# The last two of 22 inner column tiles of a feed-forward block, computed by rows and turned by transposing transfers

## The chip, the cores and the metric

One core of one Trainium2 chip runs the whole program in one launch. The metric is the device time of one execution in microseconds; the kernel before has a median of 1212.53 us over three runs (1212.32 to 1212.62). The engines named below are TensorE (PE, with its weight loads as PEld), VectorE (DVE), ScalarE (ACT), GpSimd (POOL) and SyncE (SP), which issues most transfers from memory.

## The reference, cut to what matters

The trunk has two layers of three sub-blocks each, on 256 tokens of width 1024, all in float32. Two sub-blocks of each layer are feed-forward blocks (FFNs), four in all:

```python
def _swiglu(x, w1, w3, w2):
    return (jax.nn.silu(x @ w1) * (x @ w3)) @ w2

for l in range(DEPTH):
    h = _swiglu(x, ffn_w1[l, 0], ffn_w3[l, 0], ffn_w2[l, 0])
    x = _layernorm(ALPHA * x + 0.5 * h, ln_g[l, 0], ln_b[l, 0])
    ...
```

`w1` and `w3` are 1024 x 2816 and `w2` is 2816 x 1024. The inner width of 2816 is 22 tiles of 128 columns. The mixer between the two FFNs isn't touched by the change.

## The kernel before, in words

Every float32 product is made of three products in a reduced 32-bit format (fp32r): each operand is cut into a high part (a copy on ScalarE) and a low part (operand minus high part, on VectorE), and high x high, high x low and low x high are summed in a bank of PSUM. Weights come from memory in loads of 1 MB (128 partitions x 2048 numbers) on SP's queue, into a ring of four buffers named `raw`. `stream` (L155) issues one such load, and cuts it in two pieces of 1024 columns into a ring of eight high (`whi`) and eight low (`wlo`) buffers. `step` numbers the loads; the number is the priority by which a planner puts the instructions of all engines but TensorE in order, and `behind(ins)` lets an instruction stand only after `ins` on its engine. TensorE runs in the order written. All engines take their instructions in the planned order.

A first matrix is computed in one of two ways:

- By rows (`gemm_rows`, L406): 128 tokens of x are the stationary operand and 512 columns of weights stream past, so tokens lie on partitions. Five blocks of four tiles each (20 of the 22 tiles) go this way. A block has 96 matmuls of 512. Its result h = silu(x w1) * (x w3) has to be turned, because the second matrix needs the inner dimension on partitions: `front` (L695) makes Silu on ScalarE and the product on VectorE, ScalarE splits the 32-bit words in two planes of 16 bits (`planes`, L702), SP issues a transposing transfer (L704) into `turned`, and `columns` (L681) later joins the planes on ScalarE (L688) and cuts the result into high and low parts (`keep`, L673).
- By columns (`gemm_a2`, L273): 128 columns of weights are the stationary operand and x streams past, the high and low part side by side in 512 columns; so the result lies turned already. High weights take 512 columns (x high and x low, L283), low weights 256 (x high, L290). ScalarE copies one half of each bank out (L291), VectorE adds it to the other (L293); then come Silu (L721) and the product (L722). The last two tiles (20 and 21) go this way in the loop at L717, with all four `side` banks, and their `keep` follows at once.

The second matrix (L740 on) sums over the 22 tiles of h in pairs. Five pairs (tiles 4 to 13) go through a seven-product scheme with combined weights (`stream_s`, L340: S0 to S4 in this text, seven products of three matmuls on seven banks); VectorE and ScalarE make the combinations and their high (`shi`) and low (`slo`) parts. The pairs (0,1) and (2,3) are plain loads (`plain_pair`, L732: P0 and P1), computed behind S0 and S1. The last four pairs, tiles 14 to 21, are held until the end, when the banks of the output are finished one by one: 24 matmuls of 512 for each. TensorE's order is S0, P0, S1, P1, S2, S3, S4, held. The layer norm (`Norm`) follows; two row vectors of it are fetched once one element of the last h tile is written (L505).

Of the kernel before, what the change touches and what calls it, by code (L numbers as in the profile page):

```python
# [11 lines left out]
F32 = mybir.dt.float32  # L12
# [28 lines left out]
EPS = 1e-5  # L41
# [17 lines left out]
def trunk(ctx, tc, x, xT, w13a, w13b, w2s, w2p, wb, wqk, wa, wbr, wo, gateb, sgug, sgub, sguwT, sgubias, lam, diffg,  # L59
# [18 lines left out]
    def name(s):  # L78
        serial[0] += 1
        return f"{s}_{serial[0]}"  # L80
# [21 lines left out]
    def t512(s, n=2):  # L102
        return tmp.tile([P, 512], F32, tag="main", name=name(s), bufs=n)

    def s512(s, n=4):
        return tmp.tile([P, 512], F32, tag="side", name=name(s), bufs=n)
# [39 lines left out]
            for task in list(tasks):  # L146
                turn(task)

    latest, added, emptied, silu, turned_by, early = [None, None], [None], [None], [None], [None], [None]

    def behind(ins):

# [2 lines left out]
    def stream(src, width=CH, sub=HC, lent=(), after=(None, None)):  # L155

        step()
        raw = raw_pool.tile([P, CH], F32, tag="raw", name=name("raw"))  # L160
        nc.sync.dma_start(raw[:, :width], src)
        out = []
        for o in range(0, width, HC):
            if o // HC in lent:
                hi, lo = ([act.tile([P, 512], F32R, tag="slot", name=name(n)) for _ in range(2)] for n in ("lhi", "llo"))
                at = [(hi[j], lo[j]) for j in range(2)]
            else:
                hi = hi_pool.tile([P, HC], F32R, tag="hi", name=name("whi"))
                lo = lo_pool.tile([P, HC], F32R, tag="lo", name=name("wlo"))
                at = [(hi[:, p : p + sub], lo[:, p : p + sub]) for p in range(0, HC, sub)]  # L170
            for p, (h, w) in zip(range(0, HC, sub), at):
                r = raw[:, o + p : o + p + sub]
                with behind(latest[0] if o // HC in lent else early[0] or latest[0]):
                    copied = A.activation(h, r, AF.Copy)  # L174
                if o // HC in lent:
                    early[0] = copied.ins
                with behind(after[o // HC] or latest[1]):
                    V.tensor_tensor(out=w, in0=r, in1=h.bitcast(F32), op=ALU.subtract)  # L178
            out.append((hi, lo))
        return out  # L180
# [470 lines left out]
    def ffn(l, f, i, norm, following=None):  # L651
# [21 lines left out]
        def keep(q, qa):  # L673
            if q in SQ:
                mixed(q, qa)
            else:
                split(p_hi[q], p_lo[q], qa)
# [3 lines left out]
        def columns(ins):  # L681
            while waiting:
                k0, tt = waiting.pop(0)
                h = tmp.tile([P, 2, 512], F32, tag="columns", name=name("columns"), bufs=1)
                to = h.bitcast(U16).rearrange("p q (k u t w) -> p (q k) u t w", k=2, u=2, w=2)
                for t in range(NT):
                    with behind(ins):
                        A.activation(to[:, :, t], tt[:, t].bitcast(U16).rearrange("p (w c t) -> p c t w", w=2, c=FB),  # L688
                                     AF.Copy)
                for j in range(2):  # L690
                    keep((k0 + 2 * j, k0 + 2 * j + 1), h[:, j])
                if norm is None and k0 == 0:
                    beside(setup(h[:, 0, :1]), 0)

        def front(k0):  # L695
# [12 lines left out]

            return rows

        if norm is None:
            gemm_first([w13b[l, f, 0, 0], w13b[l, f, 1, 0]], front(0))
        else:
            gemm_b2([w13b[l, f, 0, 0], w13b[l, f, 1, 0]], xh, xl, front(0), norm=norm)
        for n in range(1, NB):
            gemm_rows([w13b[l, f, m, n] for m in range(2)], xh, xl, front(n * FB), (bank, side_bank)[n % 2])
        for j in range(FR, FT, 2):  # L717
            qa = s512("qa")
            for m, z in gemm_a2([w13a[l, f, j - FR + m] for m in range(2)], both, lambda m: t512("silu"), bank=side_bank):
                s = z[:, :T]  # L720
                silu[0] = A.activation(s, s, AF.Silu).ins  # L721
                V.tensor_tensor(out=qa[:, m * T : (m + 1) * T], in0=s, in1=z[:, T:], op=ALU.mult)  # L722
                columns(silu[0])
            keep((j, j + 1), qa)
        ln = Norm(l, i, 2.0 * ALPHA, 4.0 * EPS, qa[:, :1], last)
        S = {n: side_bank() for n in (3, 7, 4)}
        S.update({n: bank() for n in (1, 2, 5, 6)})
        ends = {(0, 0): [(S[2], 0, 512)], (0, 1): [(S[3], 0, 512)], (1, 0): [(S[4], 0, 512)],
# [11 lines left out]
        for n, q in enumerate(SQ):  # L740
            pair, w = stream_s(w2s[l, f, n], pair)
            for b in (1, 2, 5, 6, 3, 7, 4):
                three(S[b], *s_op[q][b], *w[b], n == 0, n == NS - 1 and b in (1, 5, 6, 7))
            beat(1.75)
            if n < len(PQ) - HELD:
                plain_pair(n)
        u, v = s512("u"), s512("v")
        A.activation(u, S[6], AF.Copy)
        for m in range(HELD // 2):
# [265 lines left out]
def _layout(i):  # L1015
    c = np.ascontiguousarray
    L = DEPTH
    f = {k: np.asarray(v) for k, v in i.items()}
    x = f["x"].reshape(T, D)
    o = {"x": x, "xT": c(x.reshape(T, KT, P).transpose(2, 1, 0)).reshape(P, KT * T)}  # L1020

    def cols(w):

        k, n = w.shape[-2:]
        w = w.reshape(*w.shape[:-2], k // P, P, n // P, P)
        a = w.ndim
        return w.transpose(*range(a - 4), a - 2, a - 3, a - 4, a - 1)

    def pairs(w):

        w = cols(w)
        lead = w.shape[:-4]
        n = w.shape[-4]
        w = w.reshape(*lead, n // 2, 2, P, KT, P)
        a = w.ndim
        return c(w.transpose(*range(a - 4), a - 3, a - 4, a - 2, a - 1)).reshape(*lead, n // 2, P, CH)

    def halves(w):

        k, n = w.shape[-2:]  # L1040
        w = w.reshape(*w.shape[:-2], k // P, P, n // 512, 512)
        a = w.ndim
        w = c(w.transpose(*range(a - 4), a - 2, a - 3, a - 4, a - 1))
        return w.reshape(*w.shape[:-2], (k // P) * 512)

    nb = FR * P
    w1, w3 = f["ffn_w1"], f["ffn_w3"]
    o["w13a"] = c(np.stack([cols(w1[..., nb:]), cols(w3[..., nb:])], axis=4)).reshape(L, 2, FT - FR, P, CH)
    o["w13b"] = c(np.stack([halves(w1[..., :nb]), halves(w3[..., :nb])], axis=2))
    w2 = f["ffn_w2"].reshape(L, 2, FT, P, 2, 512)  # L1050

    def blocks(at):

        return c(np.stack([w2[:, :, k, :, h] for k, h in at], axis=3)).reshape(L, 2, P, CH)

    o["w2s"] = c(np.stack([blocks(((a, 0), (a, 1), (b, 1), (b, 0))) for a, b in SQ], axis=2))
    now, late = PQ[: len(PQ) - HELD], PQ[len(PQ) - HELD :]
    o["w2p"] = c(np.stack([blocks(((a, 0), (b, 0), (a, 1), (b, 1))) for a, b in now]
                          + [blocks([(k, h) for q in late[2 * m : 2 * m + 2] for k in q])
                             for h in range(2) for m in range(HELD // 2)], axis=2))  # L1060
    u, v, q, k, val, ga, gb = (f["w_in"][:, :, s * D : (s + 1) * D] for s in range(7))
    o["wb"] = np.stack([halves(w) for w in (v, val)], axis=1)
    o["wqk"] = np.stack([pairs(w) for w in (q, k)], axis=2)
    o["wa"] = np.stack([pairs(w) for w in (u, ga, gb)], axis=1)
    o["wbr"] = pairs(f["w_branch"])
    o["wo"] = halves(f["w_out"])
    o["gateb"] = c(f["gate_b"].reshape(L, 2, KT, P).transpose(3, 0, 1, 2))
    o["sgug"], o["sgub"] = f["sgu_ln_g"], f["sgu_ln_b"]
    o["sguwT"] = c(f["sgu_w"].transpose(0, 3, 1, 2)).reshape(L, P, GROUPS * P)
    o["sgubias"] = f["sgu_b"].reshape(L, GROUPS * P)  # L1070
    o["lam"] = f["lam"]
    o["diffg"] = c(f["diff_ln_g"].T)
    o["lng"], o["lnb"] = f["ln_g"], f["ln_b"]
    for k in ("lng", "lnb"):
# [26 lines left out]
```

## Time and profile before

| what | value |
|---|---|
| median of three runs | 1212.53 us |
| the profiled execution | 1213.05 us |
| its span in the trace | 1211.3 us |
| TensorE busy | 1203.7 us (99%), 5961 matmuls |
| VectorE busy | 942.9 us (78%) |
| ScalarE busy | 857.4 us (71%) |
| DMA engines, main queue | 59.9% of 16 engines |

A row of a group of instructions reads: line, engine, operation, output <- inputs, shape, count | busy time in all, mean ns of one | idle time of the engine just before, and what ended it. In a timeline, the first two numbers are start and length in us, and a bracket tells idle time before it and what ended it. A matmul's recorded length is from its issue to its end; since matmuls overlap, what one costs is the distance of starts.

### The profile page before, as it was taken

The numbers are of one execution on the slowest core, as the hardware profiler recorded it, in microseconds if no ns is written. First come the engines' busy times: TensorE is split into PE (matmuls) and PEld (weight loads), VectorE is DVE, ScalarE is ACT, GpSimd is POOL, SyncE is SP. The second block draws the span as 40 slices with busy tenths as digits, with TensorE's granted clock in tenths as the row PEclk, the third lists the DMA queues.
The fourth block names the chain that finished last, engine by engine and source line by source line (L and its number), as shares of the span: only waits on it lengthen the run. The fifth ranks groups of instructions, "written<-read, shape, count | busy, mean of one in ns | idle before, by whom it ended". The sixth has DMA issues, their size and how long they took to land.

```text
span 1211.3 us, 16542 instructions
## 1 busy us (share of the span) xinstructions
PE 1203.7 (99%) x5961; PEld 1011.3 (83%) x5961; DVE 942.9 (78%) x1540; ACT 857.4 (71%) x1384; POOL 91.1 (8%) x184
## 2 busy tenths in 40 slices
PE   9999999999999999999999999999999999999998
PEld 8888888888888878888888888888888888888886
DVE  6658998885696876579985679989766877757797
ACT  7677677679865595776776776776898556867761
POOL 0100000233300000000000000003331000000000
PEclk9999999999999999999999999999999999999999
DMA  8985665655764658665668665766648456677551
GB/s 321 323 261 174 211 249 208 227 177 166 232 227 164 217 178 282 191 192 218 229 216 270 195 176 207 254 223 199 213 139 273 176 174 217 201 259 210 184 202 47
DMA packets 101346, 257.00 MB, mean 212 GB/s; under 512 B 66528, under 2 KB 67600, under 8 KB 74640
## 3 DMA queue, kind: packets, MB, share of 16 engines
q1 hardware_dynamic: 97296, 243.03, 59.9%
q0 software_dynamic: 3536, 12.13, 3.2%
q8 instruction: 46, 0.75, 0.3%
q10 hardware_dynamic: 432, 0.79, 0.2%
q14 instruction: 36, 0.29, 0.1%
HBM read 235.47 MB, written 1.05 MB: 195 GB/s over the span
## 4 chain that ended last, share of the span: by engine, by line
PE 91%; DVE 4%; ACT 3%; issue 1%; DMA 0%; SPq 0%; POOL 0%; DVEq 0%; ACTq 0%; POOLq 0%
PE bank L271 35%; PE sbank L271 24%; PE bank L283 16%; PE bank L290 8%; PE sbank L283 2%; PE bank L446 2%; PE sbank L290 1%; PE sbank L829 1%; DVE wlo L178 1%; PE sbank L961 1%; ACT pp L839 0%; DVE nwa L248 0%; ACT xf L638 0%; ACT whi L174 0%; PE sbank L878 0%
## 5 line engine op out<-in xcount | busy, mean ns | idle before, releaser
L178 DVE TENSOR_TENSOR wlo<-raw,whi 128x1024 fp32r<-128x1024 f32 (+1 forms) x396 | 436.6, 1125 | 144.5 <-ACT whi L174 113.9
L174 ACT ACTIVATE whi<-raw 128x1024 fp32r<-128x1024 f32 (+1 forms) x396 | 372.9, 971 | 124.4 <-PE bank L283 43.2
L271 PE MATMUL bank<-whi,x 128*128 128x512 f32 x840 | 263.3, 390 | 0.0
L271 PEld LDWEIGHTS bank<-whi,x 128*128 128x128 f32 x840 | 157.7, 188 | 32.9 <-DVE gz L293 0.2
L271 PE MATMUL bank<-wlo,x 128*128 128x512 f32 x420 | 163.5, 389 | 0.0
L271 PE MATMUL sbank<-whi,x 128*128 128x512 f32 x512 | 158.9, 389 | 0.0
L283 PE MATMUL bank<-x,whi 128*128 128x512 f32 x640 | 156.0, 394 | 0.0
L283 PEld LDWEIGHTS bank<-x,whi 128*128 128x128 f32 x640 | 117.1, 188 | 26.3 <-issue 2.3
L271 PEld LDWEIGHTS sbank<-whi,x 128*128 128x128 f32 x512 | 96.1, 188 | 20.0
L353 ACT ACTIVATE shi<-raw 128x1024 fp32r<-128x1024 f32 (+1 forms) x80 | 73.4, 946 | 51.7 <-DVE raw L368 26.4
L271 PE MATMUL sbank<-wlo,x 128*128 128x512 f32 x256 | 99.6, 389 | 0.0
L355 DVE TENSOR_TENSOR slo<-raw,shi 128x1024 fp32r<-128x1024 f32 (+1 forms) x80 | 85.4, 1088 | 14.1 <-ACT shi L353 13.3
L271 PEld LDWEIGHTS bank<-wlo,x 128*128 128x128 f32 x420 | 78.9, 188 | 16.0
L290 PE MATMUL bank<-x,wlo 128*128 128x256 f32 x640 | 85.9, 285 | 0.0
L290 PEld LDWEIGHTS bank<-x,wlo 128*128 128x128 f32 x640 | 81.6, 191 | 2.2
L291 ACT ACTIVATE r<-bank 128x256 f32<-128x256 f32 x112 | 41.6, 377 | 24.0 <-PE bank L290 24.0
L271 PEld LDWEIGHTS sbank<-wlo,x 128*128 128x128 f32 x256 | 48.1, 188 | 9.9
L271 PE MATMUL sbank<-whi,hhi 128*128 128x512 f32 x144 | 56.3, 391 | 0.0
L271 PE MATMUL sbank<-whi,hlo 128*128 128x512 f32 x144 | 56.1, 390 | 0.0
L271 PE MATMUL sbank<-wlo,hhi 128*128 128x512 f32 x144 | 56.0, 389 | 0.0
L506 POOL DMA_DIRECT2D bc<-in_lng x6 | 3.2, 530 | 696.2 <-DVE bc L505 696.2
L702 ACT ACTIVATE planes<-silu 128x1024 uint16<-128x1024 uint16 x40 | 42.0, 1053 | 7.3 <-DVE silu L701 6.2
(247 smaller groups left out, 1999.1 us busy)
## 6 DMA issues: line engine op xcount, KB each, us to landing
raw<-in_w13b SPq DMA_DIRECT2D x76, 1024.0 KB, 5.4
raw<-in_w2p SPq DMA_DIRECT2D x24, 1024.0 KB, 4.9
raw<-in_wa SPq DMA_DIRECT2D x24, 1024.0 KB, 5.4
raw<-in_w2s SPq DMA_DIRECT2D x20, 1024.0 KB, 4.9
raw<-in_wb SPq DMA_DIRECT2D x16, 1024.0 KB, 5.3
raw<-in_wqk SPq DMA_DIRECT2D x16, 1024.0 KB, 4.8
raw<-in_wbr SPq DMA_DIRECT2D x16, 1024.0 KB, 4.9
raw<-in_w13a SPq DMA_DIRECT2D x8, 1024.0 KB, 4.8
```

The costliest lines, as they stand in the source:

```text
L174: copied = A.activation(h, r, AF.Copy)
L178: V.tensor_tensor(out=w, in0=r, in1=h.bitcast(F32), op=ALU.subtract)
L271: PE.matmul(ps, xx, w, start=start and n == 0, stop=stop and n == 2)
L283: PE.matmul(b[-1], hi[:, k * P : (k + 1) * P], xc(k), start=k == 0, stop=False)
L290: PE.matmul(b[n][:, :T], lo[:, k * P : (k + 1) * P], xc(k)[:, :T], start=False, stop=k == KT - 1)
L291: emptied[0] = A.activation(r[:, s], b[n][:, T:], AF.Copy, scale=scale).ins
L353: A.activation(h, r, AF.Copy)
L355: V.tensor_tensor(out=w, in0=r, in1=h.bitcast(F32), op=ALU.subtract)
L446: PE.matmul(ps[t][m], x[:, j, o + t * P : o + (t + 1) * P], y, start=k0 + j == 0 and o == 0 and y is hi, stop=k0 + j == KT - 1 and y is lo)
L702: A.activation(pk.rearrange("p (w k) -> p w k", w=2), s.bitcast(U16).rearrange("p (k w) -> p w k", w=2), AF.Copy)
L829: PE.matmul(banks[m][:, j * nk : (j + 1) * nk], rows(qT, m, j, t * P, P), rows(kT, m, j, 0, nk), start=True, stop=True)
L961: PE.matmul(b[:, j * T + t * P : j * T + (t + 1) * P], vg[t][:, g // 4, s], wsT[g // 4][:, s], start=True, stop=True)
```

## The change

Tiles 20 and 21 are computed by rows too. Their weights are laid out anew: 256 columns of w1 and 256 of w3 side by side, so that one bank of 512 holds both for 128 tokens. A function `narrow` takes the place of the loop: two loads of 1 MB as before, 48 matmuls of 512 on two side banks, then for each half of the tokens a Silu of 256 columns, a product, a plane split and a transposing transfer of half the size of a row block's. `columns` learns to take a turned tile of one pair, and the step for the last pair is called within the second matrix after P1, behind the last copy of P1 on ScalarE (`copied`). The joins of tiles 16 to 19 come behind the Silu of the second half of the tokens, where they came behind the Silu of tile 20. The norm's row vectors hang on the new `s`.

```diff
@@ stream @@
                 with behind(latest[0] if o // HC in lent else early[0] or latest[0]):
-                    copied = A.activation(h, r, AF.Copy)
+                    done = A.activation(h, r, AF.Copy)
+                copied[0] = done.ins
@@ columns @@
                 k0, tt = waiting.pop(0)
+                nq = 2 if k0 < FR else 1
                 h = tmp.tile([P, 2, 512], F32, tag="columns", name=name("columns"), bufs=1)
-                to = h.bitcast(U16).rearrange("p q (k u t w) -> p (q k) u t w", k=2, u=2, w=2)
+                to = h[:, :nq].bitcast(U16).rearrange("p q (k u t w) -> p (q k) u t w", k=2, u=2, w=2)
                 for t in range(NT):
                     with behind(ins):
-                        A.activation(to[:, :, t], tt[:, t].bitcast(U16).rearrange("p (w c t) -> p c t w", w=2, c=FB),
-                                     AF.Copy)
-                for j in range(2):
+                        A.activation(to[:, :, t], tt[:, t, : nq * T].bitcast(U16).rearrange("p (w c t) -> p c t w",
+                                                                                             w=2, c=2 * nq), AF.Copy)
+                for j in range(nq):
                     keep((k0 + 2 * j, k0 + 2 * j + 1), h[:, j])
@@ ffn @@
+        def narrow():
+
+            tt = act.tile([P, 2, 512], F32, tag="val", name=name("turned"), bufs=2)
+            ps = [side_bank() for _ in range(NT)]
+            for c in range(2):
+                for n, piece in enumerate(stream(w13a[l, f, :, c * CH : (c + 1) * CH])):
+                    for t in range(NT):
+                        rows_b(ps[t], t, 4 * c + 2 * n, piece, xh, xl, KT)
+            for t in range(NT):
+                s, pk = t512("silu"), s512("planes")[:, :T].bitcast(U16)
+                silu[0] = A.activation(s[:, :T], ps[t][:, :T], AF.Silu).ins
+                V.tensor_tensor(out=s[:, :T], in0=s[:, :T], in1=ps[t][:, T:], op=ALU.mult)
+                planes(pk, s[:, :T])
+                nc.sync.dma_start_transpose(out=tt[:, t, :T].bitcast(U16).rearrange("p (c t) -> p c t", c=4), in_=pk)
+            columns(silu[0])
+            waiting.append((FR, tt))
+            return s
...
-        for j in range(FR, FT, 2):
-            qa = s512("qa")
-            for m, z in gemm_a2([w13a[l, f, j - FR + m] for m in range(2)], both, lambda m: t512("silu"), bank=side_bank):
-                s = z[:, :T]
-                silu[0] = A.activation(s, s, AF.Silu).ins
-                V.tensor_tensor(out=qa[:, m * T : (m + 1) * T], in0=s, in1=z[:, T:], op=ALU.mult)
-                columns(silu[0])
-            keep((j, j + 1), qa)
-        ln = Norm(l, i, 2.0 * ALPHA, 4.0 * EPS, qa[:, :1], last)
+        s = narrow()
+        ln = Norm(l, i, 2.0 * ALPHA, 4.0 * EPS, s[:, :1], last)
...
             if n < len(PQ) - HELD:
                 plain_pair(n)
+            if n == len(PQ) - HELD - 1:
+                columns(copied[0])
@@ _layout @@
-    o["w13a"] = c(np.stack([cols(w1[..., nb:]), cols(w3[..., nb:])], axis=4)).reshape(L, 2, FT - FR, P, CH)
+    o["w13a"] = halves(np.concatenate([w1[..., nb:], w3[..., nb:]], axis=-1))[:, :, 0]
```

More of the change, by code (lines that the diff above doesn't have):

```diff
@@ L147, in finish_tasks @@
                 turn(task)
-    latest, added, emptied, silu, turned_by, early = [None, None], [None], [None], [None], [None], [None]
+    latest, added, emptied, silu, turned_by, early, copied = [None, None], [None], [None], [None], [None], [None], [None]
     def behind(ins):
@@ L173, in stream @@
                 with behind(latest[0] if o // HC in lent else early[0] or latest[0]):
-                    copied = A.activation(h, r, AF.Copy)
+                    done = A.activation(h, r, AF.Copy)
+                copied[0] = done.ins
                 if o // HC in lent:
-                    early[0] = copied.ins
+                    early[0] = done.ins
                 with behind(after[o // HC] or latest[1]):
```

## The prediction

> **What bounds the kernel now.** I read the page's busy times first, then TensorE's list of waits, then the chain that ended last around the edited stage, then busy time by window.
>
> ```profile
> span 1211.3 us, 16542 instructions
> PE 1203.7 (99%) x5961; PEld 1011.3 (83%) x5961; DVE 942.9 (78%) x1540; ACT 857.4 (71%) x1384; POOL 91.1 (8%) x184
> ```
>
> ```profile
> PE sbank L458 <- DVE warm L454: 1.0, 1, 1.0
> PE sbank L588 <- DVE xtok L574: 1.0, 1, 1.0
> PE sbank L633 <- DVE xtok L556: 0.8, 2, 0.4
> PE bank L271 <- DVE x L234: 0.5, 3, 0.2
> PE sbank L592 <- ACT minus L590: 0.2, 1, 0.2
> ```
>
> TensorE is busy 1203.7 of 1211.3 us, and all its recorded waits are 3.5 us: 1.0 at the warm-up, 1.2 in the last norm, and 0.8 + 0.5 = 1.3 us in the middle, all at norms. No wait belongs to the edited stage. So the time is the number of columns that TensorE streams, plus a fixed part for each matmul.
>
> The chain through the second of the four feed-forward blocks (FFN 2) shows the stage. Columns are start, length, what:
>
> ```profile
> 493.04 21.76 PE sbank L271 x96
> 514.80 21.76 PE bank L271 x96
> 536.56 7.25 PE sbank L283 x32
> 543.82 3.83 PE sbank L290 x32
> 547.65 0.47 PE bank L271 x2
> ```
>
> The first two rows are row blocks of four tiles (96 matmuls of 512), on either set of banks. The next two are the column stage that the change replaces: 32 matmuls of 512 with the high weights and 32 of 256 with the low ones. The last row is the start of the second matrix. By window, all four stages look alike, three of them shown (PE, PEld, DVE, ACT, POOL busy, clock, DMA share, GB/s); the last two rows are the stages after it, in FFN 2:
>
> ```profile
> 114.74:125.82 11.08, 11.08 (x65) 9.83 (x65) 9.82 (x16) 9.91 (x13) 0.00 (x0) 1.00 0.50 143
> 536.56:547.65 11.09, 11.09 (x66) 9.84 (x65) 9.83 (x16) 9.91 (x13) 0.00 (x0) 1.00 0.47 143
> ...
> 1135.53:1146.62 11.09, 11.09 (x65) 9.84 (x65) 9.83 (x16) 9.91 (x13) 0.00 (x0) 1.00 0.51 144
> 547.65:582.36 34.71, 34.71 (x154) 28.73 (x154) 34.17 (x42) 22.61 (x29) 1.05 (x2) 1.00 0.57 206
> 553.73:578.70 24.97, 24.97 (x112) 20.69 (x111) 24.56 (x27) 15.10 (x17) 0.00 (x0) 1.00 0.57 206
> ```
>
> TensorE is full in all of them, at clock 1.00. But from 553.73 to 578.70 VectorE is nearly full too (24.56 of 24.97 us): this is the one place near the edit where another engine could take over. ScalarE has 9.9 us to spare there, the DMA engines 43%.
>
> **TensorE, part by part.** Removed: 4 x 11.09 (once 11.08) = 44.35 us. Added per block: two loads x two halves x two token halves x two k x three products = 48 matmuls of 512, in the same order and form as a row block, so 48 x 21.76/96 = 48 x 0.2267 = 10.88 us; four times, 43.52. The streamed columns are equal (32 x 512 + 32 x 256 = 48 x 512 = 24,576). What goes is the fixed part of 16 matmuls. From the two column rows, 7.25/32 = 226.6 ns for 512 and 3.83/32 = 119.7 ns for 256 give 0.4176 ns a column and 12.8 ns fixed; 16 x 12.8 = 0.205 us a block, which agrees with 11.09 - 10.88 = 0.21. **Term: -0.83 us.** The price is bounded closely, since both sets of banks ran row blocks in 21.76.
>
> The Trainium skill, "TensorE: Matmul & The Clock Gate", section "Wait — 56ns, not 53.3ns?", gives a warm matmul N columns at 2.4 GHz plus about 2.5 ns; by that the 16 matmuls would be worth 0.04 us a block and the sum -0.16. The rows above disagree (226.6 ns, where it has 215.7), and I go by the rows.
>
> **The read-outs.** Durations by form, over the whole kernel:
>
> ```profile
> L688 ACT ACTIVATE columns<-turned 128x1024 uint16<-128x1024 uint16 x40 | 44.9, 1171 | 0.0
> L702 ACT ACTIVATE planes<-silu 128x1024 uint16<-128x1024 uint16 x40 | 42.0, 1053 | 7.3 <-DVE silu L701 6.2
> ...
> L233 ACT ACTIVATE hhi<-columns 128x512 fp32r<-128x512 f32 x20 | 12.5, 623 | 0.0
> ...
> L291 ACT ACTIVATE r<-sbank 128x256 f32<-128x256 f32 x16 | 6.0, 375 | 0.0
> ...
> L721 ACT ACTIVATE silu<-silu 128x256 f32<-128x256 f32 x8 | 3.4, 419 | 1.0 <-DVE silu L293 1.0
> ```
>
> ```profile
> L293 DVE TENSOR_TENSOR silu<-sbank,r 128x256 f32<-128x256 f32 x16 | 6.4, 420 | 0.0
> ...
> L722 DVE TENSOR_TENSOR qa<-silu 128x256 f32<-128x256 f32 x8 | 3.4, 420 | 0.0
> L234 DVE TENSOR_TENSOR hlo<-qa,hhi 128x512 fp32r<-128x512 f32 x4 | 2.8, 691 | 0.1
> ```
>
> VectorE per block: four additions and two multiplications go (6 x 0.42 = 2.52), two multiplications come (0.84): **-1.68 us**, and the 0.69 of the low half of h moves to a later place. ScalarE: four copies and two Silu go (1.50 + 0.84 = 2.34); two Silu (0.84), two plane splits and two joins of 128x512 in 16 bits come. No row has a 16-bit copy of 512; it lies between half of the 1024 rows (0.53 and 0.59) and all of them (1.05 and 1.17); I take 0.62, by the copy of equal element count. So 0.84 + 4 x 0.62 = 3.3, **+1.0 us** (ends +0.7 and +2.9). Neither is on the path, because TensorE waits for neither now; the cover is tested below.
>
> Banks: the column stage fills all four side banks and the second matrix asks for them back; the row stage fills two, read out by the same time. Weight buffers: a column load's low halves are used only from 543.82 on, so their buffers come free last; by rows a pair is freed every 2.72 us. The last high half stays 10.88 - 7.25 = 3.6 us longer; the first low half goes 7.25 + 3.83/4 - 2.72 = 5.5 us sooner. VectorE's 0.5 us wait for such a low buffer (below) should shrink. Loads: the two weight loads now have a row stride, as the row blocks' have (5.4 us to land, where this one has 4.8); both were issued within 4.94 us of 501.69, and TensorE first used them at 536.56, so 0.6 us is hidden.
>
> ```profile
> 501.69 4.94 SPq L161 DMA_DIRECT2D raw<-in_w13a  x2
> ```
>
> ```profile
> raw<-in_w13b SPq DMA_DIRECT2D x76, 1024.0 KB, 5.4
> ...
> raw<-in_w13a SPq DMA_DIRECT2D x8, 1024.0 KB, 4.8
> ...
> turned<-planes SPq DMA_TRANSPOSE x40, 3.9
> ```
>
> **The moved step.** The last pair's columns now go Silu, product, planes, two transposing transfers on SP's queue, two joins on ScalarE, high copy, low difference; the last four wait until P1 has been copied (the second matrix's loads come in the order S0, P0, S1, P1, S2, S3, S4; S is a combined load, P a plain one). TensorE's last row matmul would end near 547.4; with 0.3 for the release, Silu, product and planes (0.42 + 0.42 + 0.62) the second transfer is ready near 549.3, or near 553 if the previous block's joins (2 x 1.17 and two high copies, 1.25) go first. On SP's queue the next loads of the second matrix stood at 547.91 and 556.20:
>
> ```profile
> 547.91 0.33 SPq L344 DMA_DIRECT2D raw<-in_w2s  x1
> ...
> 556.20 0.33 SPq L344 DMA_DIRECT2D raw<-in_w2s  x1
> ```
>
> Ahead of the first, the transfers would delay it by about 2 us; that load was not copied before 556.7, so it has that time. Landing took 3.9 us in the median, so the joins can run from 553.2 or, at the late end, from 556.9; the copies of P1 ended at 556.8 (554.82 + 1.99). The pair itself is needed at the earliest late in the 24 held matmuls after 582.36, some 25 us on. What matters is what stands behind the joins on ScalarE: copies for S2, then S3 and S4, and with them VectorE's chain.
>
> ```profile
> 554.82 1.99 ACT L174 ACTIVATE whi<-raw 128x1024 fp32r<-128x1024 f32 x2
> 556.71 2.27 ACT L353 ACTIVATE shi<-raw 128x512 fp32r<-128x512 f32 x3
> ```
>
> ```profile
> 544.81 1.23 DVE L178 TENSOR_TENSOR wlo<-raw,whi 128x1024 fp32r<-128x1024 f32 x1 [0.49 <-PE sbank L290]
> ...
> 558.36 2.42 DVE L355 TENSOR_TENSOR slo<-raw,shi 128x512 fp32r<-128x512 f32 x3
> ...
> 576.20 2.52 DVE L355 TENSOR_TENSOR slo<-raw,shi 128x1024 fp32r<-128x1024 f32 x2
> ```
>
> ```profile
> 579.70 0.39 PE L271 MATMUL bank<-slo,shh 128*128 128x512 f32 x1
> ```
>
> The tightest point is S4's last low half: ready at 576.20 + 2.52 = 578.72, used at 579.70, **0.98 us of slack**. The joins put 2 x 0.62 + 0.62 = 1.86 us on ScalarE ahead of S2. If all of it came through, TensorE would wait 1.86 - 0.98 = 0.88 us a block, 3.5 in all; with joins at the long end (1.17 each) 2.96 - 0.98 = 2.0 a block, 7.9 in all. Against it stand VectorE's 1.68 us less work ahead and ScalarE's 9.9 us of idle time. At the other end, a gain, the earlier VectorE could remove the 1.3 us of waits at norms. I take 0, since the relief is about as large as the delay and the slack comes on top.
>
> **Sum.** -0.83 us. The profiled execution took 1213.05 us (span 1211.3 and 1.75 around it), so 1212.22; it ran 0.52 above the median 1212.53, so beside that **1211.7 us**, 0.07% less. What a measurement of this kernel can tell from no change is about 0.2%, or 2.4 us.
>
> **Rivals.**
>
> *The chain of low halves slips a little.* The 3.5 us above without relief: 1212.53 - 0.83 + 3.5 = 1215.2. For it: VectorE 98% busy from 553.73. Against it: the 1.68 us.
>
> *ScalarE is held by the transfer: slower.* In the view of the norm's turned tile, ScalarE did stand still for such a landing, 1.0 us each of five times:
>
> ```profile
> L628 ACT ACTIVATE xf<-sent x10: 1180/1186/1190, 180.8 to 1038.3; 128x1024 uint16<-128x1024 uint16 x10
> its engine sat idle before it (us, times) until:
>   DMA sent<-planes: 5.0, 5
> ```
>
> If the transfers are queued behind the load at 556.20, they land 0.33 + 3.9 later, at 560.4; the joins and high copy end at 562.3, S2's first copy (half a load, 0.6) at 562.9, where VectorE began at 558.36: 4.5 late, less 0.98, 3.5 us of TensorE waiting a block, 14.2 in all: **1225.9**. It decides once the delay passes 0.98 us, and counts as slower (over 0.2%) from (2.4 + 0.83)/4 = 0.8 more. Against it: the planes are ready 3 to 7 us before that load goes out, so a planner has no cause to put them behind it. The Trainium skill speaks against the change here: the same page, section "Architectural detail: the array is 16× 32×32, not 1× 128×128", has ScalarE take its instructions strictly in order. The five waits agree with that.
>
> *The norms' waits go too:* -0.83 - 1.3 = -2.1, **1210.4**. For it: less VectorE work before them. Against it: those waits hang on the norm's own steps, 45 us later.
>
> *The fixed part isn't saved:* the 12.8 ns is worked out from two forms, and might be the price of the 256 form alone; then 1212.5. Against it: both row blocks ran their 96, each with its own load, in 21.76.
>
> **Chances.** Forecast 0.68; fixed part not saved 0.06; norms too 0.06; small slip 0.09, half of it over 0.2%; held ScalarE 0.05; not foreseen 0.06, of which 0.04 faster. Faster by over 0.2%: 0.04; slower: 0.045 + 0.05 + 0.02, taken as 0.12; within: 0.84. The likeliest's own range is 1211.3 to 1212.2; the one asked for reaches from the norms' case to the small slip, 1210.4 to 1215.2.
>
> **What would show it.** Right: the four stages last 10.88 us with 48 matmuls of 512; TensorE's waits stay near 3.5 us with none on low halves of S2 to S4; the first matmul of the second matrix comes 0.21 us sooner in each block; the low halves of P0 come before 544.8. Wrong: a wait of TensorE on VectorE or ScalarE after the stage, ScalarE idle for the turned tile, S4's low half later than 0.98 us before its use, or a row stage of other than 10.88 us. A change over 2.4 us either way contradicts the sum.

## The result, and the profile after

The changed kernel takes 1216.56 us in the median of 7 runs (1215.46 to 1219.69). The kernel before took 1212.78 us in the median of 7 runs on the same chip (1212.32 to 1213.84). The ratio is 1.0032, with a 95% interval of 1.0022 to 1.0041: slower by 3.8 us, where 0.8 us less was forecast. The profiled execution took 1215.97 us, for a span of 1214.2.

The first lines of the page after, then TensorE's waits (engine, line, what it waited for: us in total, times, longest):

```profile
span 1214.2 us, 16393 instructions
PE 1204.3 (99%) x5897; PEld 1007.7 (83%) x5897; DVE 935.8 (77%) x1524; ACT 861.4 (71%) x1384; POOL 90.7 (7%) x184
```

```profile
PE bank L272 <- DVE slo L356: 1.7, 2, 0.9
...
PE sbank L589 <- DVE xtok L575: 1.0, 1, 1.0
PE sbank L634 <- DVE xtok L557: 0.8, 2, 0.4
PE sbank L844 <- ACT sbank L901: 0.7, 1, 0.7
```

TensorE has 64 matmuls fewer, VectorE 7 us less to do and ScalarE 4 us more, as forecast. Two waits are new: 1.7 us for low halves of the second matrix (slo), and 0.7 us for a bank in a mixer, far from the edit.

The chain through FFN 2 (start, length, what), and the windows of the four stages by rows (length; PE, PEld, DVE, ACT, POOL busy; clock; DMA share; GB/s):

```profile
537.10 10.88 PE sbank L272 x48
547.98 2.72 PE bank L272 x12
```

```profile
114.85:125.73 10.88, 10.88 (x49) 9.01 (x49) 10.75 (x17) 7.57 (x9) 0.00 (x0) 1.00 0.56 157
537.10:547.98 10.88, 10.88 (x50) 9.01 (x49) 10.75 (x17) 7.57 (x9) 0.00 (x0) 1.00 0.56 156
...
1135.62:1146.50 10.88, 10.88 (x50) 9.01 (x49) 10.75 (x17) 7.57 (x9) 0.00 (x0) 1.00 0.61 157
```

The stage does what it was to do: 10.88 us each time, with TensorE full. So the loss is elsewhere. Each part of the program starts with the same matmul in every kernel, so the starts in two traces can be subtracted part by part. The table is worked out in this way. It gives the length of each part in the profiled execution of before (the last part ends with TensorE's last matmul), and the difference of each other kernel to it; the experiments' names are explained below (e3, e6, e7 and e8, which aren't in the table, are told in the text).

| part, by before's time (us) | before | after | e1 | e2 | e4 | e5 | e9 | e10 | e11 |
|---|---|---|---|---|---|---|---|---|---|
| start, to 27.5 | 27.54 | +.11 | -.02 | -.32 | -.24 | -.33 | -.34 | +.43 | -.35 |
| FFN 1, to 178.4 | 150.87 | -.23 | -.23 | .00 | -.23 | -.12 | .00 | -.10 | -.23 |
| norm, to 190.3 | 11.86 | +.07 | +.01 | .00 | +.01 | +.67 | +.01 | +.63 | +.13 |
| mixer 1, to 434.3 | 244.03 | +.56 | +.72 | -.02 | +1.36 | +.85 | +1.15 | -.24 | +.50 |
| FFN 2, to 600.2 | 165.93 | -.21 | -.22 | +.01 | -.20 | -.23 | +.01 | -.20 | -.20 |
| norm, to 612.1 | 11.88 | +.02 | -.01 | -.01 | -.01 | +.09 | -.03 | -.03 | +.24 |
| FFN 3, to 778.1 | 165.97 | -.23 | -.23 | .00 | -.23 | -.23 | .00 | -.23 | -.23 |
| norm, to 790.0 | 11.87 | .00 | +.02 | +.02 | +.01 | .00 | -.01 | +.01 | +.01 |
| mixer 2, to 1033.2 | 243.29 | -.01 | -.02 | +.03 | -.01 | -.01 | +.25 | +.86 | +.49 |
| FFN 4 and last norm, to 1207.3 | 174.08 | +2.79 | +.48 | +1.36 | +.49 | -.23 | -.02 | -.25 | -.23 |
| sum | 1207.33 | +2.89 | +.49 | +1.07 | +.94 | +.46 | +1.03 | +.88 | +.12 |

FFN 1 to 3 each gain 0.21 to 0.23 us. Mixer 1 loses 0.56, and FFN 4 loses 2.79. The losses in FFN 4 and mixer 1 have nothing in common, as the experiments show.

**FFN 4.** The chain that ended last, followed back from the end, comes to S4's low half, and from there through VectorE and ScalarE to a transfer that GpSimd asked for. First before, then after:

```profile
1176.56 2.72 PE bank L271 x12
1179.28 2.04 PE sbank L271 x9
1181.32 5.44 PE bank L271 x24
```

```profile
1148.61 0.01 POOLq L507
1148.62 4.92 DMA bc<-in_lng
...
1153.64 0.10 ACT bc L526
...
1154.61 0.85 ACT shi L354
...
1156.60 1.90 ACT whi L174 x2
...
1180.12 1.23 DVE slo L356
...
1181.40 0.73 PE bank L272 x2
...
1184.21 5.44 PE bank L272 x24
```

The transfer brings the row of the last norm's scale, and the instruction at 1153.64 multiplies it by -0.5 on ScalarE. That instruction exists only in the last block. ScalarE's own timeline (start, length, line, operation, output and input; in brackets idle time before it and its releaser) shows what stood where. Before:

```profile
1150.05 1.28 ACT L531 ACT_TABLE_LOAD   x1
...
1152.29 1.06 ACT L353 ACTIVATE shi<-raw 128x1024 fp32r<-128x1024 f32 x1 [0.21 <-DVE raw L368]
1153.25 1.99 ACT L174 ACTIVATE whi<-raw 128x1024 fp32r<-128x1024 f32 x2
1155.60 1.06 ACT L525 ACTIVATE bc<-bc 128x1024 f32<-128x1024 f32 x1 [0.35 <-DMA bc<-in_lng]
```

After:

```profile
1150.82 1.28 ACT L532 ACT_TABLE_LOAD   x1
...
1153.64 1.06 ACT L526 ACTIVATE bc<-bc 128x1024 f32<-128x1024 f32 x1 [0.81 <-DVE hlo L235]
1154.61 2.00 ACT L354 ACTIVATE shi<-raw 128x1024 fp32r<-128x1024 f32 x2
1156.50 1.99 ACT L174 ACTIVATE whi<-raw 128x1024 fp32r<-128x1024 f32 x2
```

Before, the scaling stood behind the copies of S1 and P1; after, it stands ahead of them and waits for its row. P1's copies start 3.25 us later (1156.50 against 1153.25). VectorE, which makes the low halves from these copies, has nothing to do meanwhile:

```profile
1150.83 0.69 DVE L235 TENSOR_TENSOR hlo<-columns,hhi 128x512 fp32r<-128x512 f32 x1 [2.44 <-ACT hhi L234]
1152.87 0.69 DVE L235 TENSOR_TENSOR hlo<-columns,hhi 128x512 fp32r<-128x512 f32 x1 [1.34 <-ACT hhi L234]
1155.68 2.36 DVE L356 TENSOR_TENSOR slo<-raw,shi 128x1024 fp32r<-128x1024 f32 x2 [2.12 <-ACT shi L354]
```

The idle times are 5.9 us in sum, more than the 1.68 us of work that the change took away. The bracket of the scaling names the second of these differences, which ended at 1152.87 + 0.69 = 1153.56. But the scaling doesn't use its result, and the chain puts the row's transfer there, which landed at 1148.62 + 4.92 = 1153.54.

VectorE's order at the end of S4 differs as well. In before its last two low halves stand one behind the other; in after a sum into the output rows stands between them:

```profile
1179.53 0.68 DVE L541 SCALAR_TENSOR_TENSOR xtok<-xtok,bank 128x512 f32<-128x512 f32 x1
```

The two low halves stand together again in e1, e4 and e5, but not in e3. What this sum alone costs there wasn't measured; it is part of the loss of FFN 4. TensorE then waits:

```profile
1179.66 0.50 PE L272 MATMUL bank<-slo,shh 128*128 128x512 f32 x1 [0.91 <-DVE slo L356]
```

The list of waits counts only the idle time behind a matmul's recorded end, 1.7 us. By the distance of starts, this matmul comes 1.41 us after the one ahead of it and the second one that waits comes 1.17 us after its own, where others come every 0.23; so these two cost 2.1 us, and the rest of what FFN 4 lost goes in tenths at other matmuls of S2 to S4.

### The profile page after: what moved, and what is told of

Read it like the earlier page. It is cut to its first block, busy times and chain, and to the rows that moved or that the text cites. A ratio compares the mean times of both kernels' runs of the same rounds, so it can differ in the third digit from the quotient of the medians.

```text
span 1214.2 us, 16393 instructions
## 1 busy us (share of the span) xinstructions
PE 1204.3 (99%) x5897; PEld 1007.7 (83%) x5897; DVE 935.8 (77%) x1524; ACT 861.4 (71%) x1384; POOL 90.7 (7%) x184
## 4 chain that ended last, share of the span: by engine, by line
PE 69%; issue 19%; DVE 5%; ACT 3%; DMA 2%; POOL 1%; DVEq 0%; ACTq 0%; POOLq 0%
PE bank L272 26%; PE sbank L272 21%; PE bank L284 11%; PE bank L291 6%; PE bank L447 2%; PE sbank L844 1%; DMA bc<-in_lng 1%; DVE slo L356 1%; ACT whi L174 1%; DMA wsT<-in_sguwT 0%; DMA bc<-in_sgug 0%; PE sbank L893 0%; ACT gate L939 0%; DVE nwa L249 0%; DVE xtok L557 0%
## 5 line engine op out<-in xcount | busy, mean ns | idle before, releaser
L272 PE MATMUL sbank<-whi,x 128*128 128x512 f32 x640 | 199.0, 389 | 0.0
L272 PEld LDWEIGHTS sbank<-whi,x 128*128 128x128 f32 x640 | 120.1, 188 | 24.9
L272 PE MATMUL sbank<-wlo,x 128*128 128x512 f32 x320 | 124.5, 389 | 0.0
L272 PEld LDWEIGHTS sbank<-wlo,x 128*128 128x128 f32 x320 | 60.1, 188 | 12.5
L690 ACT ACTIVATE columns<-turned 128x1024 uint16<-128x1024 uint16 (+1 forms) x48 | 50.5, 1089 | 0.3 <-DMA turned<-planes 0.2
```

The costliest lines, as they stand in the source:

```text
L272: PE.matmul(ps, xx, w, start=start and n == 0, stop=stop and n == 2)
L690: A.activation(to[:, :, t], tt[:, t, : nq * T].bitcast(U16).rearrange("p (w c t) -> p c t w", w=2, c=2 * nq), AF.Copy)
```

## The experiments

All ratios are to before on the same chip; there before was 1212.78 us (for e1, e2, e3 and e5), 1212.81 (e4, e6, e7 and e8) and 1212.83 (e9 to e11).

### FFN 4: what holds ScalarE

**The scaling set behind the copies of S2** (e1, from after):

```diff
-                A.activation(self.g, self.g, AF.Copy, scale=-0.5)
...
+            if last and n == 2:
+                with behind(copied[0]):
+                    A.activation(ln.g, ln.g, AF.Copy, scale=-0.5)
```

> Edit: only in the last FFN, the copy on ScalarE that scales the norm's row by -0.5 stands two combined loads later; in the changed kernel it stands ahead of S1's and P1's copies, where it starts at 1153.64 after 0.81 us of idle time and takes about 1 us. Theory (the last norm's own instructions on ScalarE, no longer covered, hold S1's and P1's copies): the wait of TensorE on S4's low halves in the last FFN falls from 2.8 us to about 1.0, time 1213.0 to 1214.3 us. Rival (the two joins of the new turned pair are what delays the copies): no change, about 1216.5. Second rival (general slip of VectorE in all four FFNs): no change.

1214.81 us (1213.57 to 1217.74), ratio 1.0015 (1.0007 to 1.0024). The wait falls from 1.7 to 0.3 us, and FFN 4 from +2.79 to +0.48, so the theory holds for the stage. The time is 0.5 us above the range expected; the profiled execution, at 1213.57, is the fastest of its runs.

**The copies of P1 forced behind the scaling** (e2, from before, where nothing else differs):

```diff
-                A.activation(self.g, self.g, AF.Copy, scale=-0.5)
+                self.scaled = A.activation(self.g, self.g, AF.Copy, scale=-0.5).ins
...
+            if last and n == 1:
+                latest[0] = ln.scaled
```

> Edit to the kernel before: P1's two copies in the last FFN are made to stand behind the scaling copy, which waits for its row until 1155.6. Theory: P1's copies start near 1156.5 instead of 1153.25, VectorE then idles about 2.5 us, and less 0.98 us of slack TensorE waits about 1.5 us in the last FFN: 1214.0 to 1215.0 us, with none of the change's row stage in the kernel. Rival (joins): there are none here, so no change, 1212.8.

1214.13 us (1213.48 to 1214.44), ratio 1.0010 (1.0001 to 1.0019). The same wait of TensorE appears in a kernel without the change, and FFN 4 loses 1.36 us:

```profile
PE bank L271 <- DVE slo L355: 0.8, 2, 0.4
```

So the order alone costs this much. It is less than in after, probably since here only P1 is held and not S1. The time came as expected; the wait, expected at 1.5 us, is 0.8.

**The row loaded earlier** (e4, from after; the two requests go out before the stage by rows):

```diff
...
+        rows = (bc_load(lng[l, i], ident[:, :1]), bc_load(lnb[l, i], ident[:, :1])) if last else None
         s = narrow()
-        ln = Norm(l, i, 2.0 * ALPHA, 4.0 * EPS, s[:, :1], last)
+        ln = Norm(l, i, 2.0 * ALPHA, 4.0 * EPS, s[:, :1], last, rows)
```

> After, with the two row loads of the last norm issued before the narrow block, so that the row is there long before the scaling copy. Theory (in the last feed-forward the planned order sets the scaling of the norm's row, which waits for the row's transfer, ahead of S1's and P1's copies): the scaling no longer holds the copies for the transfer; the wait of TensorE on S4's low half (1.7 us in after) falls to 0.5 or less, the last feed-forward block ends near 1181.8 instead of 1184.2, and the time is 1213.3 to 1214.8. Rival (the held copies come from the later read-outs and joins, not from the row): the wait stays at 1.5 or more and the time at 1215.5 or more.

1215.52 us (1213.98 to 1217.76), ratio 1.0023 (1.0014 to 1.0032). FFN 4 did as expected (wait 0.4, +0.49 us, as in e1 by another way). The time is above what was expected and reaches what the rival gave, but the rival's wait of 1.5 us or more isn't there; the profiled execution, at 1213.98 the fastest of its runs, has its largest loss in mixer 1, +1.36.

**The late joins set behind S2** (e3, from after; they are called after S3, and run behind S2's copies):

```diff
-            if n == len(PQ) - HELD - 1:
+            if n == 3:
                 columns(copied[0])
```

> Edit: the joins and the high copy of the last pair (1.25 + 0.62 us on ScalarE) are called after S3 instead of after P1, in all four FFNs. Theory: the last norm's instructions still hold S1 and P1, so TensorE's wait in the last FFN only falls from 2.8 to 1.5 to 2.3 us: 1215.0 to 1216.1 us. Rival (joins are the cause): the wait goes, 1212.0 to 1213.3 us.

1216.22 us (1214.84 to 1218.10), ratio 1.0025 (1.0013 to 1.0036). The wait on low halves stays at 1.7 us, and FFN 4 still loses 2.18. The time is 0.1 us above the range expected. So the joins, which the prediction had weighed at 0.88 us a block, aren't the main cause: behind S2 instead of ahead of it, they change FFN 4 by 0.61 us and the other three by 0.01 at most.

**Scaling and table load both set late** (e5, from after: the scaling as in e1, and the square root that loads the table at n == 3), and **the same in before** as a control (e8):

```diff
-                with behind(silu[0]):
-                    A.activation(sm("first", 1), mask[:, :1], AF.Sqrt)
...
+            if last and n == 3:
+                with behind(copied[0]):
+                    A.activation(sm("first", 1), mask[:, :1], AF.Sqrt)
```

> Edit: as e1_scale_late, and the last norm's table load (1.28 us) and the one-element square root behind it stand three combined loads later too. Theory: nothing of the last norm is left ahead of S1's and P1's copies, the last FFN is like the other three, TensorE waits for no low half, and the gain of 0.2 us a block stays: 1211.9 to 1212.7 us, a little under the kernel before. Rival (general slip, or joins): 1215 to 1216.5.

> Before, with the same late place for the last norm's scaling and table load as in e5_norm_late. Theory (in before these instructions stand in idle time of ScalarE): no change, 1212.4 to 1213.0. Rival (the late place is a gain of its own, also without the change): 1212.2 or less.

e5: 1213.51 us (1212.48 to 1217.08), ratio 1.0008 (0.9999 to 1.0016). e8: 1212.83 us (1212.31 to 1213.45), ratio 1.0000 (0.9991 to 1.0008). In e5 the wait is gone, and FFN 4 gains 0.23 like the other three:

```profile
1177.02 2.72 PE bank L272 x12
...
1181.78 5.44 PE bank L272 x24
```

So the loss in FFN 4 comes apart: 2.79 - 0.48 = 2.3 us for the scaling that waits, 0.48 + 0.23 = 0.7 us for the table load of 1.28 us ahead of the same copies, and under both the -0.23 of the forecast. In before the place of these two instructions costs nothing. e5 as a whole missed the expected 1211.9 to 1212.7: it lost 0.85 us in mixer 1 and 0.67 in the norm ahead of it.

**One transposing transfer in place of two** (e7, from e5, the two of the stage by rows merged into one of full size):

```diff
-                nc.sync.dma_start_transpose(out=tt[:, t, :T].bitcast(U16).rearrange("p (c t) -> p c t", c=4), in_=pk)
...
+            flat = tt[:, 0]
+            nc.sync.dma_start_transpose(out=flat.bitcast(U16).rearrange("p (c t) -> p c t", c=8), in_=pks)
```

> The version with the norm's own instructions set later (as in e5_norm_late), and the two half-size transposing transfers of the narrow block merged into one of full size. Theory: one transfer fewer per block than in e5_norm_late moves the slow issue of SP once more; where it leaves the small transfers of mixer 1 alone, the wait of 0.7 us there is gone and the time is 1212.0 to 1212.9, below e5_norm_late by 0.6 to 1.2 us. If the slow issue stays on the chain, 1213.2 to 1213.8. The merged transfer waits for both read-outs, about 1.6 us later than the first half did, which 6 us of row stage behind it should hide.

1216.38 us (1214.26 to 1218.95), ratio 1.0029 (1.0018 to 1.0040). Missed: the wait in mixer 1 stays, and the norms between the blocks now wait three times on ScalarE:

```profile
PE bank L272 <- ACT x L234: 1.0, 3, 0.4
```

### Mixer 1: a wait that no edited line makes

In mixer 1 SP issues small transfers that swap halves of a tile (swap), one after another, and TensorE's chain needs each. SP's timeline and the row of DMA queue q8 for the same 1.5 to 2 us (queue: packets, MB, share) put the slow one in different places. Before, two windows:

```profile
237.97 1.15 SPq L801 DMA_DIRECT2D swap<-z  x2
...
253.94 2.34 SPq L801 DMA_DIRECT2D swap<-z  x2
```

```profile
q8 instruction: 1, 0.02, 4.5%
```

The queue's row is that of the second window, 254 to 256 us; from 237.5 to 239 there was no packet on q8. After, near 238 us:

```profile
237.92 1.63 SPq L816 DMA_DIRECT2D swap<-z  x2
```

```profile
q8 instruction: 1, 0.02, 3.8%
```

Where two issues take 1.15 us, they take 1.63 or 2.34 with a packet of q8 in the window, and the slow one has moved from 254 to 238 us. The product on GpSimd that uses the swapped tile then starts 0.4 us later, and VectorE's difference beside it takes longer. Before, then after:

```profile
241.92 1.30 POOL L805 TENSOR_TENSOR swap<-swap,sin_t 128x512 f32<-128x512 f32 x1 [7.72 <-DMA swap<-z]
...
242.67 1.64 DVE L178 TENSOR_TENSOR wlo<-raw,whi 128x1024 fp32r<-128x1024 f32 x1
```

```profile
242.32 1.28 POOL L820 TENSOR_TENSOR swap<-swap,sin_t 128x512 f32<-128x512 f32 x1 [8.07 <-DMA swap<-z]
...
242.63 2.05 DVE L179 TENSOR_TENSOR wlo<-raw,whi 128x1024 fp32r<-128x1024 f32 x1
```

This lateness of 0.41 us is not yet the loss; what became of it is told below, ahead of e9.

**Is it the number of transposing transfers on SP's queue?** (e6, from before; two more of half size in each block, which nothing reads)

```diff
+        pad = s512("pad").bitcast(U16)
+        for t in range(NT):
+            nc.sync.dma_start_transpose(out=pad[:, t * 512 : (t + 1) * 512].rearrange("p (c t) -> p c t", c=4),
+                                        in_=qa.bitcast(U16)[:, t * 512 : (t + 1) * 512])
```

> Before, with two more transposing transfers of half size on SP's queue in each feed-forward, which nothing reads. Theory (the number of transposing transfers on that queue sets at which transfer SP's slow issue of over 1 us falls, and in after it falls on a small transfer of mixer 1 that TensorE's chain needs): the slow issue moves from transfer 102 (254.6 us) to one between 238 and 243 us, the wait on sbank in mixer 1 appears with about 0.7 us, and the time is 1213.2 to 1213.9, 0.5 to 1.1 us above before. Rival (the wait in mixer 1 comes from something else in after): no such wait and 1212.5 to 1213.0.

1212.90 us (1212.68 to 1215.18), ratio 1.0003 (0.9994 to 1.0012). No: the slow issue stays at the same transfer (254.06 us, 1.61 us long), and TensorE's wait there is 0.2 us. That theory fell.

The queue q8 carries 46 packets in either kernel:

```profile
q8 instruction: 46, 0.75, 0.2%
```

That is 0.75 MB / 46 = 16 KB a packet, and 5897 / 46 = 128 matmuls, each with its weight load. In before the packets come every 105 to 151 matmuls. The Trainium skill, "Advanced Engine Details and Errata", section "ISA Cache", gives a cache line of 16 KB, or 256 instructions; 128 matmuls and 128 loads agree. So q8 looks like TensorE's program coming in, and 16 matmuls fewer ahead of a place set its pieces to other moments. Over the 13 traces, 35 of the 37 issues over 0.8 us (transposing transfers and the first 100 us left out) have a packet of q8 that starts no more than 0.7 us before or during them; of the other 3291 it is 161, or 5%. So nearly every slow issue has met a piece, while most issues that meet one aren't slow (161 of 196).

The loss in mixer 1 is made 35 us behind the slow issue, at 273.5 us, and doesn't come from it directly. VectorE's 0.41 us are made good by 256 us, where its next low half waits for TensorE in either kernel (after is 0.04 us ahead here). What is lost begins at GpSimd's product behind that, which waits for the last of four transfers. Before, then after, each with the time of that transfer from issue to landing:

```profile
256.16 1.23 DVE L178 TENSOR_TENSOR wlo<-raw,whi 128x1024 fp32r<-128x1024 f32 x1 [1.11 <-PE bank L290]
...
258.43 1.29 POOL L805 TENSOR_TENSOR swap<-swap,sin_t 128x512 f32<-128x512 f32 x1 [10.25 <-DMA swap<-z]
...
DMA to landing us min/median/max: 2.0/2.0/2.0
```

```profile
256.12 1.23 DVE L179 TENSOR_TENSOR wlo<-raw,whi 128x1024 fp32r<-128x1024 f32 x1 [0.70 <-PE bank L291]
...
258.94 1.29 POOL L820 TENSOR_TENSOR swap<-swap,sin_t 128x512 f32<-128x512 f32 x1 [10.52 <-DMA swap<-z]
...
DMA to landing us min/median/max: 3.1/3.1/3.1
```

The trace tells of a landing in sixteen signals. In before all are there at 258.31 us. In after fifteen are there at 257.59 and the last comes at 258.70, and a piece of q8 is under way from 256.65 to 257.61. From here on VectorE and ScalarE are 0.55 us late, up to the matmul at 273.5 us that waits. In the seven kernels with this wait of 0.7 us (after, e1, e3, e4, e5, e7 and e9) the last signal of this transfer comes 1.1 to 1.9 us behind the fifteenth, with a piece that starts 1.1 to 1.3 us after the issue. In the other six it comes within 0.1 us, and no piece starts between issue and landing. GpSimd's product is 0.55 to 1.34 us late in the seven, within 0.1 us of what mixer 1 loses there, but for e7 (1.13 of 1.75). So the slow issue at 238 us shows that the pieces come at other moments, and the wait hangs on a landing near 258 us that goes with another piece. That this piece holds the signal back, rather than only coming with it, rests on these 13 traces and on e9.

**The program shifted by 16 matmuls and nothing else** (e9, from before):

```diff
-    warm = const.tile([P, P], BF16, name="warm")
+    warm = const.tile([P, T], BF16, name="warm")
...
-    for _ in range(WARM):
-        PE.matmul(b[:, :P], warm, warm, start=True, stop=True)
+    for n in [T] * 16 + [P] * 5:
+        PE.matmul(b[:, :n], warm[:, :P], warm[:, :n], start=True, stop=True)
```

> Before, whose 37 idle matmuls at the very start (on a tile of zeros, whose results nothing reads) are merged into 21 of the same total width, so that TensorE's program is 16 matmuls shorter ahead of everything, as the change makes it ahead of mixer 1, and nothing else differs. Theory (TensorE's program comes in by 16 KB pieces, one for some 128 matmuls; 16 fewer ahead of mixer 1 set the piece that came at 254.46 us of before, and the one at 237.27, to other moments, and the one that comes near 238.3 lengthens SP's issue of a small transfer that TensorE's chain needs): SP's slow issue moves from its transfer number 102 to number 93, TensorE waits about 0.7 us in mixer 1 as in after, the stretch from 190 to 312 us lasts 0.5 to 0.8 us longer than in before, and the time is 1213.1 to 1213.8. Rival (another part of the change makes that wait): the slow issue stays at number 102, no such wait, 1212.5 to 1213.0.

1214.10 us (1211.85 to 1214.59), ratio 1.0008 (0.9999 to 1.0017). A kernel without any of the change gets its wait in mixer 1, by the length of a warm-up loop 230 us earlier:

```profile
PE sbank L829 <- ACT sbank L886: 0.7, 1, 0.7
```

```profile
237.64 1.52 SPq L801 DMA_DIRECT2D swap<-z  x2
```

The slow issue is at transfer 91, which is 93 less the two transposing transfers of FFN 1 that before doesn't have, so it is the transfer that was slow in after. The stretch from 190 to 312 us lasts 1.11 us longer, where 0.5 to 0.8 was expected, and the median is 0.3 above the range. The ratio's interval just includes 1, so the claim rests on the trace. The transfer issued at 255.23 us takes 3.9 us to land, with a piece of q8 under way: the cause that was expected holds, and its path doesn't, since the wait hangs on this landing. That the start is 0.34 us shorter here isn't the cause: it is 0.32 shorter in e2, whose mixer 1 is as in before.

**The shift undone, or doubled, in e5** (e10: 53 warm-up matmuls; e11: 69; both of the old total width):

```diff
-    for _ in range(WARM):
-        PE.matmul(b[:, :P], warm, warm, start=True, stop=True)
+    for n in [64] * 32 + [P] * 21:
+        PE.matmul(b[:, :n], warm, warm[:, :n], start=True, stop=True)
```

> The version e5_norm_late (after, with the last norm's own instructions set later), with the idle matmuls at the start split into 53 of the same total width, 16 more, so that TensorE's program has the same number of matmuls ahead of mixer 1 as in before. Theory: the slow issue goes back to SP's transfer number 104 or so (102 of before, and the two transposing transfers), the wait of 0.7 us in mixer 1 is gone, the stretch from 190 to 312 us lasts as in before within 0.2 us, and the time is 1212.0 to 1212.8 (four blocks each 0.2 us shorter, nothing lost). Rival: the wait stays, 1213.2 to 1213.9.

> As e10_late_16_more, with 69 idle matmuls of the same total width, 32 more. Theory: the pieces of TensorE's program come at still other moments, so the slow issues of SP stand at other transfers than in before, in after and in e10_late_16_more; whether one of them is needed by TensorE's chain isn't known beforehand, so the time is 1212.0 to 1212.8 if none is and 0.5 to 1 us more for each that is. Rival (the pieces have no part in it): the slow issue at number 93 as in e5_norm_late and 1213.2 to 1213.9.

e10: 1214.33 us (1213.69 to 1215.20), ratio 1.0013 (1.0004 to 1.0022). e11: 1213.37 us (1212.68 to 1215.11), ratio 1.0007 (0.9998 to 1.0016). In e10 the slow issue is back at 256 us (number 105, one transfer on from that of before), the wait is 0.2 us, and mixer 1 is 0.24 shorter than in before. But the time expected of it was missed, because other places now lose: mixer 2 +0.86, the norm after FFN 1 +0.63 and the start +0.43. In e11 number 93 is not slow and the wait at 273.5 us is gone; but both mixers lose half a microsecond, mixer 1 near 349 us, with no slow issue in it. Whether the pieces make these other losses isn't shown. None of these versions is shown to be faster than before.

## Why the prediction was wrong

**TensorE's term was right.** Four stages of 10.88 us with 48 matmuls, 0.21 to 0.23 us less in each of FFN 1 to 3, and in FFN 4 too once the norm is out of the way (e5: -0.23). The fixed part of a matmul is real, and the rivals "the fixed part isn't saved" and "the norms' waits go too" are out: the waits at the norms are the same 0.8 and 1.0 us.

**The read-outs were sized well.** The 16-bit forms that had no row took 0.68 us (joins) and 0.63 us (plane splits) each, where 0.62 was chosen:

```profile
L690 ACT ACTIVATE columns<-turned 128x512 uint16<-128x512 uint16 x8 | 5.2, 679 | 0.3 <-DMA turned<-planes 0.2
...
L185 ACT ACTIVATE planes<-silu 128x512 uint16<-128x512 uint16 x8 | 5.0, 625 | 3.5 <-DVE silu L724 3.5
```

**The step that failed is the moved step, at "I take 0".** In FFN 2, whose rows it quoted, it holds: S4's last low half ends at 576.58 + 2.52 = 579.10, 0.38 us later than before (of which 0.33 is where the second matrix starts, 547.98 against 547.65), and is used at 580.01. So 0.91 us of slack is left of 0.98, and TensorE doesn't wait.

```profile
576.58 2.52 DVE L356 TENSOR_TENSOR slo<-raw,shi 128x1024 fp32r<-128x1024 f32 x2
```

The working took FFN 2 for all four blocks. FFN 4 lost 3.0 us beside the forecast instead: 2.3 for the scaling that waits and 0.7 for the table load. There ScalarE also has the last norm's table load (1.28 us) and scaling (1.06), and the scaling waits for a row that GpSimd requests only after the last product of the stage. The change moved that product, and with it the request, from 1151 to 1148.6 us, and the planned order then put the scaling ahead of S1's and P1's copies, whose buffers the stage by rows frees later (the last high half is used until 1146.5, where it was until 1142.8). Why the plan chose this is argued from those times; that the order costs what it costs is shown by e1, e2 and e5. The norm's construction is in the diff, one line below the replaced loop, and the table load stood in FFN 4's own trace.

**The rival that came true was "ScalarE is held by the transfer", with the wrong transfer.** It looked only at the turned tile, as did its "against", and had a chance of 0.05. The mechanism fits: a copy stream standing behind one instruction that waits for a landing, past the slack (0.98 us in FFN 2; 0.84 in FFN 4, from 1177.83 to 1178.67 in before). The Trainium skill, "TensorE: Matmul & The Clock Gate", section "Architectural detail: the array is 16× 32×32, not 1× 128×128", has ScalarE take its instructions strictly in order, and the row at 1153.64 agrees: the copies behind it started at 1154.61, and in e1, where it doesn't stand ahead of them, at 1152.63.

**No step foresaw mixer 1.** The prediction counted what 16 matmuls cost in time, and not that TensorE's program is shorter by them. e9 shows that this alone makes the wait, and the landings above by what path.

**What stays open.** The profiled execution of after lost 2.89 us to that of before, the medians differ by 3.78. The changed kernels also spread more: after over 4.2 us in 7 runs, e7 over 4.7, before over 1.5 in its 7. One profile of e3, at 1218.10, lost 2.66 us in mixer 2 with a second wait like mixer 1's, so the rest may be more such meetings; with one profile of each kernel this isn't shown. Open as well are the +0.63 to +0.67 in the norm after FFN 1 of e5, e7 and e10, and the losses of e10 and e11 in other places.

## What to carry to other kernels

A slack that is read in one repetition of a block holds for that block: look at the last one too, where the epilogue's own loads and table switches share the engines. When a planner or a queue fixes the order, ask of each moved instruction which others hang on its result, here a row request behind a tile's last product, since their place in the order moves with it. Under about 0.1% the number of instructions is itself a variable, and a control that shifts the program without the edit tells its effect from the edit's.

## What the runs showed of the hardware that was not expected

A 16 KB piece on the queue q8 that comes around the issue of a small transfer by SP can lengthen this issue from some 0.6 us to between 0.8 and 1.9. That it lengthens it, rather than only coming with it, rests on e9, where 16 matmuls fewer at the start moved the slow issue, with a piece beside it, from 254 to 238 us. A piece that starts 1.1 to 1.3 us after the issue goes with a last landing signal that is 1.1 to 1.9 us late: the transfer ahead of GpSimd's product near 258 us landed 3.1 to 4.0 us after its issue in the seven kernels with such a piece, and some 2.0 us after it in before, e2, e6, e8 and e11.

While GpSimd's product of 128x512 runs, VectorE's difference hardly gets on. Alone it takes 1.21 us (at 237.81 in before); with 0.55 us of overlap it took 1.64, and with 0.97 us of overlap 2.05 (the rows of mixer 1 above). The Trainium skill, "GPSIMD Engine Reference", section "1. Specifications", has GpSimd's interface to the on-chip memory contend with VectorE instructions that read two inputs there; both instructions here read two, and these numbers agree.
